# Down projection of the SwiGLU blocks: splits, sums and bank readings put in program order, readings moved directly behind their product

## The chip, the cores and the metric

The kernel runs on one core of one Trainium2 chip. The metric is device time in microseconds of that core, from launch to the last output; the time of a kernel is the median of its runs. The profile is one execution taken by the hardware profiler; its times count from the start of its span.

## The reference, cut to what matters

Two decoder layers, each a SwiGLU block, a mixer (attention and retention) and a second SwiGLU block, on 512 tokens of width 1024. The change lies in the SwiGLU block, which runs four times:

```python
D_MODEL = 1024; SEQ = 512; DEPTH = 2
D_FF = ((8 * D_MODEL // 3 + 127) // 128) * 128        # 2816

def swiglu_ffn(x, w_gu, w_down):
    a, u = jnp.split(x @ w_gu, 2, axis=-1)
    return (jax.nn.silu(a) * u) @ w_down

for l in range(DEPTH):
    x = layer_norm(ALPHA * x + 0.5 * swiglu_ffn(x, ffn1_w_gu[l], ffn1_w_down[l]), ln1_g[l], ln1_b[l])
    x = layer_norm(ALPHA * x + hybrid_mixer(x, w_in[l], w_out[l], ...), ln2_g[l], ln2_b[l])
    x = layer_norm(ALPHA * x + 0.5 * swiglu_ffn(x, ffn2_w_gu[l], ffn2_w_down[l]), ln3_g[l], ln3_b[l])
```

## The kernel before

**Three matmuls for one.** Every float32 operand is split into a high part (a copy to `float32r` on ScalarE, ACT) and a low part (operand minus high part, on VectorE, DVE); `split` issues the two. `mm3` then runs high x high, high x low and low x high on TensorE (PE). A split of 128x1024 is called a unit when it is of weights: tiles `uh` and `ul`. Units live in a pool of six (`UBUFS`).

**Where weights come from.** `Weights` holds the list of all units of the program. `get` hands the next one to PE; `done` gives a buffer back and calls `pump`, which emits loads (SP queue) and splits until six are held. So in the text of the program the split of unit i + 6 stands right behind the `done` of group i (numbered as below).

**The down projection.** Behind the gate and up projections a SwiGLU block multiplies its activations `hT` (22 blocks of 128 x 512 tokens) by the down weights, into eight PSUM banks. Blocks 0 to 15 go through a seven-product scheme (Strassen's), the others directly:

- The loop over `n` in `ffn` runs products n = 0 to 6 into the bank pairs left, low, high, low, right, low, low. Each has four groups `g`, each one unit and 12 matmuls of 128x512 (`seventh`). I number the groups i = 4n + g. Between n = 5 and n = 6 stands a direct `chunk` for block 16, whose last six matmuls add to the low banks; behind n = 6 chunk 17, then the tail (blocks 18 to 21, in tiles `hr`), whose first matmuls are followed by the layer norm.
- Weights of products: `down_items`. Products n = 1, 2, 3 and 6 use the same two tiles `R` (`R_311`, `R_312` in the first block): after the split of a group (`ul` on DVE has read it), POOL issues a DMA that adds the next block of weights onto the same half tile (L369), and the unit four places later (twelve from n = 3 to n = 6) is split from that sum; n = 4 and 5 do the same with two other tiles `R`. So unit i = 10 (`uh_341`, `ul_342`, n = 2, g = 2) needs the DMA that was issued behind unit i = 6 (`ul_332`).
- Activations of products: the generator `operands`. `operand` splits one 128x1024 piece into a quarter of `xh` and `xl`, which serves two groups. `fifth` (n = 2) first makes sums: s1 = a21 - a22, then a21 = a11 - a21 and a11 = s1 - a11 in place, and splits s1. `third` (n = 4) makes one sum. The list `ahead` keeps the operands three groups in front: the code that makes `fifth(0)`, used from i = 8, stands at i = 5; `fifth(1)`, used from i = 10, at i = 7; each behind the splits of unit i + 5 in the text (`ul_342` at i = 5, `ul_346` at i = 7).
- Readings: `into` adds a finished bank pair onto `Y` in SBUF (L726, two instructions). A bank may only be written again when it has been read.

**What sets the order.** Instructions go to each engine in an order that is fixed at build time; each engine then runs its own list from front to back. A scheduler may reorder what the program issued, except instructions for which `keep_in_program_order` was called. `self.pin` decides that in `split`; it is True at the start of the program and becomes False in the first SwiGLU block, at `fp == 0`. From there on only the POOL DMAs of L369 keep their place, and the scheduler places splits, sums and readings.

Of the kernel before, what the change touches and what calls it, by code (L numbers as in the profile page):

```python
# [7 lines left out]
F32 = mybir.dt.float32  # L8
F32R = mybir.dt.float32r
AF = mybir.ActivationFunctionType  # L10
ALU = mybir.AluOpType
# [18 lines left out]
GROUPS = 4  # L30
# [64 lines left out]
class Trunk:  # L95
# [57 lines left out]
    def units(self, pool=None, tag="u", bufs=None):  # L153
# [3 lines left out]
        lo = pool.tile([P, 1024], F32R, tag=tag + "l", name=self.nm("ul"), **kw)  # L157
        return hi, lo

    def split(self, hi, lo, src):  # L160
        a = self.nc.scalar.copy(hi, src)  # L161
        b = self.nc.vector.tensor_sub(lo, src, hi.bitcast(F32))  # L162
        if self.pin:
            self.tc.keep_in_program_order(a)
            self.tc.keep_in_program_order(b)

    def mm3(self, out, a, b, start, stop, **kw):
        (ah, al), (bh, bl) = a, b
# [313 lines left out]
    def ffn(self, g_, b, out=None):  # L482
        nc, tc, W = self.nc, self.tc, self.W
        with ExitStack() as ctx:
# [99 lines left out]
            for fp in range(NFP):  # L584
                if fp == 0:
# [4 lines left out]
                    more = []  # L590
# [46 lines left out]
            def part(m, i, j):  # L637

                f = (j * GROUPS + 2 * m) * 2
                return hT[:, f : f + 4, i * 256 : (i + 1) * 256]  # L640

            def operand(src):

                k = slots[0] = (slots[0] + 2) % KC
                f = src.shape[1]
                hh, hl = (v[:, k : k + 2, :].rearrange("p k t -> p (k t)").rearrange("p (f t) -> p f t", f=f)
                          for v in (self.xh, self.xl))
                self.split(hh, hl, src)
                h = f // 2
                return [(hh[:, q * h : q * h + h], hl[:, q * h : q * h + h]) for q in range(2)]  # L650

            s1 = pool.tile([P, 4, 256], F32, tag="tlh", name=self.nm("s1"), bufs=TAIL)

            def fifth(m):

                a11, a21, a22 = part(m, 0, 0), part(m, 1, 0), part(m, 1, 1)
                nc.vector.tensor_sub(s1, a21, a22)
                nc.vector.tensor_sub(a21, a11, a21)
                nc.vector.tensor_sub(a11, s1, a11)
                return operand(s1)  # L660

            def third(m):

                nc.vector.tensor_add(part(m, 0, 1), part(m, 0, 1), part(m, 0, 0))
                return operand(part(m, 0, 1))

            def operands():
                ms = range(GROUPS // 2)
                for m in ms[1:]:
                    yield from operand(part(m, 0, 1))  # L670
                for m in ms:
                    yield from operand(part(m, 0, 0))
                for m in ms:
                    yield from fifth(m)
                for m in ms:
                    yield from operand(part(m, 0, 0))
                for m in ms:
                    yield from third(m)
                for m in ms:
                    yield from operand(part(m, 1, 0))  # L680
                chunks = operand(hT[:, FIRST : FIRST + 2, :])
                yield chunks[0]
                for m in ms:
                    yield from operand(part(m, 1, 1))
                yield chunks[1]
                for f in range(NF - TAIL, NF, 2):
                    room = pool.tile([P, 2, 2, 512], F32R, tag="hr", name=self.nm("hr"), bufs=2)
                    self.split(room[:, 0], room[:, 1], hT[:, f : f + 2, :])
                    for q in range(2):
                        yield room[:, 0, q : q + 1], room[:, 1, q : q + 1]  # L690

            def seventh(banks, u, h, new):

                for i, b_ in enumerate(banks):
                    ts = slice(i * P, (i + 1) * P)
                    for f in range(2):
                        self.mm3(b_, (h[0][:, f, ts], h[1][:, f, ts]), (u[0][:, f, :], u[1][:, f, :]),
                                 new and f == 0, False, skip_group_check=True)
                self.step()

            def down(f, u, h, t, q):
# [2 lines left out]
                self.mm3(acc[t][q], (h[0][:, 0, ts], h[1][:, 0, ts]), (u[0][:, hs], u[1][:, hs]), False, f == NF - 1,  # L704
                         skip_group_check=True)

            split = operands()
            ahead = [(hv[0][:, g], hv[1][:, g]) for g in range(2)] + [next(split)]

            def chunk(f):  # L710
                u, h = W.get(), ahead.pop(0)
                ahead.append(next(split))
                for i, (t, q) in enumerate(((0, 0), (0, 1), (1, 0), (1, 1), (2, 1), (3, 1), (2, 0), (3, 0))):
                    down(f, u, h, t, q)
                    if i % 4 == 3:
                        self.step()
                W.done()
# [4 lines left out]
            def into(banks, t0, q, scale, sign=ALU.add):  # L722

                for i, b_ in enumerate(banks):
                    y = self.Y[:, t0 + i, q * 512 : (q + 1) * 512]
                    nc.vector.scalar_tensor_tensor(out=y, in0=y, scalar=scale, in1=b_, op0=ALU.mult, op1=sign)  # L726

            for n, (banks, new, more) in enumerate((
                    (left, True, None), (low, True, (0, 0, ALPHA)), (high, True, (0, 1, ALPHA)),
                    (low, False, (0, 1, 1.0, ALU.subtract)), (right, True, None),  # L730
                    (low, False, (2, 1, ALPHA, ALU.subtract)), (low, False, None))):
                if n == 6:
                    chunk(FIRST)
                for g in range(GROUPS):
                    u, h = W.get(), ahead.pop(0)
                    ahead.append(next(split))
                    seventh(banks, u, h, new and g == 0)
                    W.done(2 if n == 0 and g == 1 else 1)
                if more:
                    into(banks, *more)  # L740
            for f in range(FIRST + 1, NF - TAIL):
                if f == FIRST + 1:
                    gb = self.load_ln(self.spool, g_, b, "S", 2)
# [397 lines left out]
```

## Time and profile before

| what | value |
|---|---|
| median of 3 runs | 1791.03 us (1787.59 to 1792.43) |
| the profiled execution: its time / its span | 1792.29 us / 1790.4 us |
| busy in the span: DVE, ACT, POOL | 1386.6, 906.4, 162.7 us |
| granted TensorE clock, mean | 0.998 |
| first down projection (225 to 355 us): PE and DVE busy of 130 us | 127.99, 103.34 us |
| L726, reading of a bank | 32 times, 674 to 682 ns |
| L369, DMA issue on POOL | 64 times, 512 KB each |

How to read the rows below: in a timeline a row has start, duration (both us), engine, line, operation and tiles; the bracket at its end gives the idle time of the engine just before it and what was taken to end it. Buffer numbers are left out there, so `ul<-R,uh` is any weight unit split from a tile `R`. `PE ps L170` is the first matmul of `mm3`, L171 the second and L172 the third. In a list of waits: who waited for whom, us in total, times, longest us. The time from launch to span (1792.29 - 1790.4 = 1.9 us) is outside the rows.

### The profile page before, as it was taken

Reading aid. Unit: us, or ns where it says so; the run is one execution under the profiler, and the core shown is the slowest. Engines: PE = TensorE matmul, PEld = TensorE weight load, DVE = VectorE, ACT = ScalarE, POOL = GpSimd, SP = SyncE. Lnnn points to the kernel's source line nnn. Section 1 sums busy time; section 2 is a strip of 40 time slices with the busy share of each in tenths; the row PEclk is TensorE's granted clock in tenths of the full one; section 3 lists DMA queues with packets and bytes.
Section 4 is the critical chain, followed back from the end, with each engine's and each line's share of the span. In section 5 each row is a group of like instructions: output and inputs, shape, how many; then the busy total and the mean of one; then the engine's idle time right before and its main releaser. Section 6 shows DMA issues by size and latency. Waiting matters only on the chain.

```text
span 1790.4 us, 29087 instructions
## 1 busy us (share of the span) xinstructions
PE 1767.3 (99%) x11978; PEld 1611.0 (90%) x11978; DVE 1386.6 (77%) x1926; ACT 906.4 (51%) x1423; POOL 162.7 (9%) x136
## 2 busy tenths in 40 slices
PE   9999999999999999999999999999999999999998
PEld 9999987887789999998799999889877899999876
DVE  7888888656767888879688887877667687888884
ACT  5455555278722455556235555553785234555550
POOL 0000031111111000012000000301011100000211
PEclk9999999999999999999999999999999999999999
DMA  6234397223222232389313324961323122244961
GB/s 188 95 102 135 120 228 172 88 83 90 52 95 71 86 127 95 95 241 181 118 58 98 106 95 165 224 175 42 99 79 94 48 95 95 95 129 131 217 136 48
DMA packets 158326, 210.07 MB, mean 117 GB/s; under 512 B 4848, under 2 KB 116208, under 8 KB 158192
## 3 DMA queue, kind: packets, MB, share of 16 engines
q1 hardware_dynamic: 140784, 174.64, 30.3%
q0 software_dynamic: 17408, 33.56, 10.5%
q8 instruction: 94, 1.54, 0.4%
q14 instruction: 40, 0.33, 0.1%
HBM read 206.09 MB, written 2.10 MB: 116 GB/s over the span
## 4 chain that ended last, share of the span: by engine, by line
PE 73%; DVE 10%; issue 7%; DMA 4%; ACT 4%; POOL 1%; SPq 0%; POOLq 0%; DVEq 0%; ACTq 0%
PE ps L170 23%; PE ps L171 23%; PE ps L172 23%; DVE ul L162 4%; DMA R<-in_ffn_w_down_dram 2%; DVE xl L162 2%; ACT uh L161 1%; PE ps L435 1%; DMA raw<-in_ffn_w_down_dram 1%; ACT sw L910 1%; DMA raw<-in_ffn_w_gu_dram 1%; ACT b L952 1%; ACT b L946 1%; DVE Y L726 1%; POOL R L369 0%
## 5 line engine op out<-in xcount | busy, mean ns | idle before, releaser
L170 PE MATMUL ps<-xh,uh 128*128 128x256 f32 (+1 forms) x1616 | 482.1, 298 | 0.0
L172 PE MATMUL ps<-xh,ul 128*128 128x256 f32 (+1 forms) x1616 | 479.1, 297 | 0.9 <-DVE ul L162 0.9
L171 PE MATMUL ps<-xl,uh 128*128 128x256 f32 (+1 forms) x1616 | 478.7, 296 | 0.2 <-DVE xl L162 0.2
L161 ACT CAST uh<-raw 128x1024 fp32r<-128x1024 f32 (+1 forms) x285 | 249.2, 894 | 247.9 <-PE ps L171 136.8
L162 DVE TENSOR_TENSOR ul<-raw,uh 128x1024 fp32r<-128x1024 f32 (+1 forms) x285 | 287.6, 1024 | 87.8 <-ACT uh L161 87.5
L170 PE MATMUL ps<-Th,uh 128*128 128x256 f32 x1152 | 319.1, 277 | 0.0
L171 PE MATMUL ps<-Tl,uh 128*128 128x256 f32 x1152 | 318.7, 277 | 0.0
L172 PE MATMUL ps<-Th,ul 128*128 128x256 f32 x1152 | 318.3, 276 | 0.0
L170 PEld LDWEIGHTS ps<-xh,uh 128*128 128x128 f32 x1616 | 307.9, 191 | 10.5 <-issue 1.6
L172 PEld LDWEIGHTS ps<-xh,ul 128*128 128x128 f32 x1616 | 307.8, 191 | 9.8 <-DVE ul L162 1.3
L171 PEld LDWEIGHTS ps<-xl,uh 128*128 128x128 f32 x1616 | 308.0, 191 | 8.4 <-DVE xl L162 0.8
L170 PE MATMUL ps<-uh,xh 128*128 128x512 f32 x672 | 265.1, 394 | 8.2 <-DVE Y L726 8.2
L171 PE MATMUL ps<-ul,xh 128*128 128x512 f32 x672 | 262.2, 390 | 0.0
L172 PE MATMUL ps<-uh,xl 128*128 128x512 f32 x672 | 261.9, 390 | 0.0
L161 ACT CAST uh<-S 128x1024 fp32r<-128x1024 f32 x144 | 151.2, 1050 | 149.0 <-PE ps L171 145.1
L162 DVE TENSOR_TENSOR ul<-S,uh 128x1024 fp32r<-128x1024 f32 x144 | 175.9, 1221 | 60.1 <-ACT uh L161 59.5
L171 PEld LDWEIGHTS ps<-Tl,uh 128*128 128x128 f32 x1152 | 216.7, 188 | 0.0
L170 PEld LDWEIGHTS ps<-Th,uh 128*128 128x128 f32 x1152 | 216.7, 188 | 0.0
L172 PEld LDWEIGHTS ps<-Th,ul 128*128 128x128 f32 x1152 | 216.3, 188 | 0.0
L369 POOL DMA_DIRECT2D R<-in_ffn_w_down_dram x64 | 77.7, 1216 | 994.7 <-DVE ul L162 959.0
L170 PEld LDWEIGHTS ps<-uh,xh 128*128 128x128 f32 x672 | 126.5, 188 | 38.2 <-DVE Y L726 9.9
L172 PEld LDWEIGHTS ps<-uh,xl 128*128 128x128 f32 x672 | 126.4, 188 | 26.6
(143 smaller groups left out, 2391.5 us busy)
## 6 DMA issues: line engine op xcount, KB each, us to landing
raw<-in_ffn_w_gu_dram SPq DMA_DIRECT2D x86, 1024.0 KB, 5.4
R<-in_ffn_w_down_dram POOLq DMA_DIRECT2D x64, 512.0 KB, 7.4
raw<-in_ffn_w_down_dram SPq DMA_DIRECT2D x20, 1024.0 KB, 5.1
raw<-in_w_in_dram SPq DMA_DIRECT2D x18, 1024.0 KB, 5.2
R<-in_ffn_w_down_dram SPq DMA_DIRECT2D x16, 1024.0 KB, 6.4
raw<-in_w_in_dram SPq DMA_DIRECT2D x8, 512.0 KB, 4.6
raw<-in_w_out_dram SPq DMA_DIRECT2D x8, 512.0 KB, 6.2
raw<-in_w_out_dram SPq DMA_DIRECT2D x4, 1024.0 KB, 4.9
```

Source lines behind the costliest of these rows:

```text
L161: a = self.nc.scalar.copy(hi, src)
L162: b = self.nc.vector.tensor_sub(lo, src, hi.bitcast(F32))
L170: mm(out, ah, bh, start=start, stop=False, **kw)
L171: mm(out, ah, bl, start=False, stop=False, **kw)
L172: mm(out, al, bh, start=False, stop=stop, **kw)
L369: self.nc.gpsimd.dma_start(src, rows(i, j, g * 256, 256), accum_op=ALU.add))
L435: nc.tensor.transpose(b[:, c * P : (c + 1) * P], src[:, c * P : (c + 1) * P], self.ident)
L726: nc.vector.scalar_tensor_tensor(out=y, in0=y, scalar=scale, in1=b_, op0=ALU.mult, op1=sign)
L910: nc.scalar.copy(sw[q * 32 : q * 32 + 32, :n], src[o * 32 : o * 32 + 32, :n])
L946: nc.scalar.activation(s[kv][:, cc, :nk], s[kv][:, cc, :nk], AF.Exp, bias=m[:, cc : cc + 1], scale=SCALE, accum_out=den[:, cc : cc + 1])
L952: nc.scalar.activation(s[kv][:, cc, :nk], s[kv][:, cc, :nk], AF.Copy, scale=den[:, cc : cc + 1])
```

## The change

`pin` is set to True ahead of the loop over `n` and back to False behind it, so that within the seven products every split, every sum of activations and every reading keeps the program's place. `fifth`, `third` and `into` call `keep` for this. And `into` moves from behind the last group's `W.done` to before it, that is ahead of the split that this `done` emits.

```diff
+    def keep(self, ins):
+        if self.pin:
+            self.tc.keep_in_program_order(ins)
+
     def split(self, hi, lo, src):
-        a = self.nc.scalar.copy(hi, src)
-        b = self.nc.vector.tensor_sub(lo, src, hi.bitcast(F32))
-        if self.pin:
-            self.tc.keep_in_program_order(a)
-            self.tc.keep_in_program_order(b)
+        self.keep(self.nc.scalar.copy(hi, src))
+        self.keep(self.nc.vector.tensor_sub(lo, src, hi.bitcast(F32)))
...
             def fifth(m):
...
-                nc.vector.tensor_sub(s1, a21, a22)
-                nc.vector.tensor_sub(a21, a11, a21)
-                nc.vector.tensor_sub(a11, s1, a11)
+                for out, p_, q_ in ((s1, a21, a22), (a21, a11, a21), (a11, s1, a11)):
+                    self.keep(nc.vector.tensor_sub(out, p_, q_))
                 return operand(s1)
...
-                nc.vector.tensor_add(part(m, 0, 1), part(m, 0, 1), part(m, 0, 0))
+                self.keep(nc.vector.tensor_add(part(m, 0, 1), part(m, 0, 1), part(m, 0, 0)))
...
+            self.pin = True
             split = operands()
...
-                    nc.vector.scalar_tensor_tensor(out=y, in0=y, scalar=scale, in1=b_, op0=ALU.mult, op1=sign)
+                    self.keep(nc.vector.scalar_tensor_tensor(out=y, in0=y, scalar=scale, in1=b_, op0=ALU.mult,
+                                                             op1=sign))
...
                     seventh(banks, u, h, new and g == 0)
+                    if more and g == GROUPS - 1:
+                        into(banks, *more)
                     W.done(2 if n == 0 and g == 1 else 1)
-                if more:
-                    into(banks, *more)
+            self.pin = False
             for f in range(FIRST + 1, NF - TAIL):
```

No instruction is added or removed; orders change on DVE, ACT and SP, and by one matmul per SwiGLU block on PE. POOL's order stays. The three places below are in the first SwiGLU block; the other three have the same rows with other buffer numbers.

**DVE around the first sum of `fifth`.** `ul_318` to `ul_344` are units i = 4 to 11, L657 to L659 the sums, `xl_78<-s1` the low part of the first operand of n = 2. Before:

```order
L162 TENSOR_TENSOR xl_78<-hT_14_145,xh_77 128x1024
L162 TENSOR_TENSOR ul_318_2767<-R_311_2700,uh_317_2766 128x1024
L657 TENSOR_TENSOR s1_328_2786<-hT_14_145 128x1024
L162 TENSOR_TENSOR ul_330_2802<-R_311_2700,uh_329_2801 128x1024
L658 TENSOR_TENSOR hT_14_145<-hT_14_145 128x4x256
L162 TENSOR_TENSOR ul_332_2821<-R_312_2702,uh_331_2820 128x1024
L162 TENSOR_TENSOR ul_334_2826<-R_312_2702,uh_333_2825 128x1024
L659 TENSOR_TENSOR hT_14_145<-s1_328_2786,hT_14_145 128x4x256
L162 TENSOR_TENSOR xl_78<-s1_328_2786,xh_77 128x1024
L162 TENSOR_TENSOR ul_336_2843<-R_311_2700,uh_335_2842 128x1024
L162 TENSOR_TENSOR ul_340_2866<-R_311_2700,uh_339_2865 128x1024
```

Of the change, from `ul_334` on (the sums are all on L659 there):

```order
L166 TENSOR_TENSOR ul_334_2826<-R_312_2702,uh_333_2825 128x1024
L166 TENSOR_TENSOR ul_336_2843<-R_311_2700,uh_335_2842 128x1024
L166 TENSOR_TENSOR xl_78<-hT_14_145,xh_77 128x1024
L166 TENSOR_TENSOR ul_340_2866<-R_311_2700,uh_339_2865 128x1024
L166 TENSOR_TENSOR ul_342_2883<-R_312_2702,uh_341_2882 128x1024
L659 TENSOR_TENSOR s1_328_2786<-hT_14_145 128x1024
L659 TENSOR_TENSOR hT_14_145<-hT_14_145 128x4x256
L659 TENSOR_TENSOR hT_14_145<-s1_328_2786,hT_14_145 128x4x256
L166 TENSOR_TENSOR xl_78<-s1_328_2786,xh_77 128x1024
L166 TENSOR_TENSOR ul_344_2905<-R_312_2702,uh_343_2904 128x1024
L166 TENSOR_TENSOR ul_346_2922<-R_311_2700,uh_345_2921 128x1024
```

Before, the first sums and `xl_78<-s1` stand between the units i = 4 to 7 and ahead of `ul_336`; in the change they stand behind `ul_342`, and the second set of sums and its `xl_78<-s1` directly behind `ul_346`. The `xl_78<-hT` that stood directly ahead of `ul_318` stands behind it in the change.

**DVE around the reading of product n = 5.** `ul_372` to `ul_378` are the units of n = 6, `ul_380` chunk 17, `ul_383` to `ul_391` and `hr` the tail. Before:

```order
L162 TENSOR_TENSOR hr_389_3302<-hT_14_145,hr_389_3302 128x1024
L162 TENSOR_TENSOR ul_370_3145<-raw_308_2671,uh_369_3144 128x1024
L162 TENSOR_TENSOR hr_396_3343<-hT_14_145,hr_396_3343 128x1024
L162 TENSOR_TENSOR xl_78<-hT_14_145,xh_77 128x1024
L162 TENSOR_TENSOR ul_372_3163<-R_311_2700,uh_371_3162 128x1024
L162 TENSOR_TENSOR ul_374_3179<-R_311_2700,uh_373_3178 128x1024
L162 TENSOR_TENSOR xl_78<-hT_14_145,xh_77 128x1024
L162 TENSOR_TENSOR ul_376_3197<-R_312_2702,uh_375_3196 128x1024
L162 TENSOR_TENSOR ul_378_3215<-R_312_2702,uh_377_3214 128x1024
L726 SCALAR_TENSOR_TENSOR Y_79<-Y_79,ps_324_2782 128x512
L726 SCALAR_TENSOR_TENSOR Y_79<-Y_79,ps_326_2784 128x512
L162 TENSOR_TENSOR ul_380_3231<-raw_308_2671,uh_379_3230 128x1024
```

Of the change:

```order
L166 TENSOR_TENSOR ul_378_3215<-R_312_2702,uh_377_3214 128x1024
L727 SCALAR_TENSOR_TENSOR Y_79<-Y_79,ps_324_2782 128x512
L727 SCALAR_TENSOR_TENSOR Y_79<-Y_79,ps_326_2784 128x512
L166 TENSOR_TENSOR ul_380_3233<-raw_308_2671,uh_379_3232 128x1024
L166 TENSOR_TENSOR xl_78<-hT_14_145,xh_77 128x1024
L166 TENSOR_TENSOR ul_383_3265<-raw_315_2737,uh_382_3264 128x1024
L166 TENSOR_TENSOR ul_385_3281<-raw_315_2737,uh_384_3280 128x1024
L166 TENSOR_TENSOR ul_388_3299<-raw_381_3236,uh_387_3298 128x1024
L166 TENSOR_TENSOR hr_389_3302<-hT_14_145,hr_389_3302 128x1024
L166 TENSOR_TENSOR ul_391_3318<-raw_381_3236,uh_390_3317 128x1024
L166 TENSOR_TENSOR hr_396_3343<-hT_14_145,hr_396_3343 128x1024
```

The reading stands behind `ul_378` in both. But the six splits of the tail (`ul_383`, `ul_385`, `ul_388`, `ul_391`, two `hr`), which before stood ahead of the reading, among the units of n = 4 and n = 5, now stand behind it.

**SP's loads around the tail.** `raw_381` holds the down weights of the last two tail units, `raw_386` and `raw_392` the first weights of the next stage, `ln` the norm's constants. Before:

```order
L358 DMA R_338_2846<-in_ffn1_w_down_dram 128x4x512
L267 DMA raw_381_3234<-in_ffn1_w_down_dram 128x2x1024
L191 DMA raw_386_3284<-in_w_in_dram 128x8x256
L448 DMA ln_395_3340<-in_ln1_g_dram 128x1024
L449 DMA ln_395_3340<-in_ln1_b_dram 128x1024
L229 DMA raw_392_3321<-in_w_in_dram 128x8x128 x2
```

Of the change:

```order
L359 DMA R_338_2846<-in_ffn1_w_down_dram 128x4x512
L449 DMA ln_395_3340<-in_ln1_g_dram 128x1024
L450 DMA ln_395_3340<-in_ln1_b_dram 128x1024
L268 DMA raw_381_3236<-in_ffn1_w_down_dram 128x2x1024
L192 DMA raw_386_3284<-in_w_in_dram 128x8x256
L230 DMA raw_392_3321<-in_w_in_dram 128x8x128 x2
```

The loads of `raw_381` and `raw_386` moved behind those of `ln`; `raw_381` now takes the buffer that `ul_380` leaves, where before it took the one that `ul_385` left.

## The prediction

> **What bounds the kernel now.** I read the page's busy times first, then the list of waits for PE, then the timeline at each of them.
>
> ```profile
> span 1790.4 us, 29087 instructions
> PE 1767.3 (99%) x11978; PEld 1611.0 (90%) x11978; DVE 1386.6 (77%) x1926; ACT 906.4 (51%) x1423; POOL 162.7 (9%) x136
> PE ps L170 <- DVE Y L726: 8.2, 4, 3.5
> ```
>
> PE is busy for 1767.3 of 1790.4 us, so a change of order can win little and lose more: work in front of PE counts only where PE stands still. Half of what PE waits for is one line: four times, once per SwiGLU block, a bank had not been read by L726 when PE came back to it. On PE, first block, then the others:
>
> ```profile
> 302.62 0.39 PE L172 MATMUL ps<-uh,xl 128*128 128x512 f32 x1
> 305.02 0.50 PE L170 MATMUL ps<-uh,xh 128*128 128x512 f32 x1 [2.01 <-DVE Y L726]
> 305.36 0.39 PE L171 MATMUL ps<-ul,xh 128*128 128x512 f32 x1
> 855.11 0.50 PE L170 MATMUL ps<-uh,xh 128*128 128x512 f32 x1 [2.04 <-DVE Y L726]
> 1189.63 0.50 PE L170 MATMUL ps<-uh,xh 128*128 128x512 f32 x1 [0.69 <-DVE Y L726]
> 1737.32 0.39 PE L172 MATMUL ps<-uh,xl 128*128 128x512 f32 x1
> 1741.21 0.80 PE L170 MATMUL ps<-uh,xh 128*128 128x512 f32 x1 [3.50 <-DVE Y L726]
> 1741.80 0.63 PE L171 MATMUL ps<-ul,xh 128*128 128x512 f32 x1
> ...
> 1744.59 0.40 PE L172 MATMUL ps<-uh,xl 128*128 128x512 f32 x1
> ```
>
> The reader is to see the starts. With the start of the stage at 233.47 (quoted below), the 306th matmul starts at 302.62: a step of 69.15 / 305 = 0.2267 us. In the first block the step of the wait is 2.40, and the next 0.34, together 2.28 too long, 0.27 more than the idle time in the bracket. Added to the brackets of the second and third block that makes 2.31 and 0.96. In the fourth, nine steps take 7.27 instead of 2.04: 5.23 lost, of which 3.5 is the wait; the rest is the clock:
>
> ```profile
> 853.00:855.00 2.00, 0.07 (x1) 0.00 (x0) 2.00 (x4) 0.00 (x0) 0.00 (x0) 1.00 0.98 309
> 1742.00:1744.00 2.00, 2.00 (x7) 1.52 (x6) 0.89 (x1) 0.00 (x0) 0.00 (x0) 0.50 0.00 0
> ```
>
> In these windows (length, then busy PE, PEld, DVE, ACT, POOL, then the granted clock) the clock stays 1.00 in a wait of 2 us and falls to 0.50 behind the one of 3.5. The late readings cost 2.28 + 2.31 + 0.96 + 5.23 = **10.8 us**: the most that the change can win.
>
> **First term, the reading.** Before, the reading of n = 5 is late because DVE is behind with its list:
>
> ```profile
> 304.29 1.27 DVE L726 SCALAR_TENSOR_TENSOR Y<-Y,ps 128x512 f32<-128x512 f32 x2
> ```
>
> Product n = 5 ended at 233.47 + 288 x 0.2267 = 298.8, PE comes back to its banks 18 matmuls (4.1 us) later, and the readings start only at 304.29. Six splits that stood ahead move behind, at 1.135 us a step (rows below) 6.8 us, more than the reading is late. Nothing else ahead of it in the new list is late, and once the product ends the two readings need some 1.3 of the 4.1 us. So the four waits go: -10.8.
>
> **Second term, what the program's order holds up.** The sums of `fifth` and `xl<-s1` stood early in DVE's list; now they stand behind `ul_342`, whose high part waits for a DMA. The start of the stage on PE in the four blocks, and the start of this high part (`uh_341` and its likes) on ACT:
>
> ```profile
> 233.47 0.39 PE L170 MATMUL ps<-uh,uh 128*128 128x512 f32 x1
> 783.53 0.39 PE L170 MATMUL ps<-uh,uh 128*128 128x512 f32 x1
> 1119.40 0.39 PE L170 MATMUL ps<-uh,uh 128*128 128x512 f32 x1
> 1668.17 0.39 PE L170 MATMUL ps<-uh,uh 128*128 128x512 f32 x1
> ```
>
> ```profile
> 247.32 1.05 ACT L161 CAST uh<-R 128x1024 fp32r<-128x1024 f32 x1 [4.26 <-PE ps L172]
> 249.87 1.05 ACT L161 CAST uh<-R 128x1024 fp32r<-128x1024 f32 x1 [1.50 <-DMA R<-in_ffn_w_down_dram]
> 252.49 1.05 ACT L161 CAST uh<-R 128x1024 fp32r<-128x1024 f32 x1 [1.57 <-DMA R<-in_ffn_w_down_dram]
> 803.32 1.05 ACT L161 CAST uh<-R 128x1024 fp32r<-128x1024 f32 x1 [1.49 <-DMA R<-in_ffn_w_down_dram]
> 1138.17 1.05 ACT L161 CAST uh<-R 128x1024 fp32r<-128x1024 f32 x1 [1.57 <-DMA R<-in_ffn_w_down_dram]
> 1688.22 1.05 ACT L161 CAST uh<-R 128x1024 fp32r<-128x1024 f32 x1 [2.66 <-DMA R<-in_ffn_w_down_dram]
> ```
>
> I call this start U, counted from the stage's: 19.02, 19.79, 18.77 and 20.05 us. (At 247.32 the page names PE, but unit i = 8 needs PE only up to group 2, done at 241.6; so there too it was the DMA.) DVE's durations and steps:
>
> ```profile
> 248.41 1.23 DVE L162 TENSOR_TENSOR ul<-R,uh 128x1024 fp32r<-128x1024 f32 x1 [3.47 <-ACT uh L161]
> 252.09 1.22 DVE L657 TENSOR_TENSOR s<-hT 128x1024 f32<-128x1024 f32 x1
> 253.23 1.22 DVE L664 TENSOR_TENSOR hT<-hT 128x1024 f32<-128x1024 f32 x1
> 254.36 1.22 DVE L162 TENSOR_TENSOR ul<-R,uh 128x1024 fp32r<-128x1024 f32 x1
> ```
>
> A low part starts 1.09 behind its high part (247.32 to 248.41); neighbours on DVE start 1.135 apart; each lasts 1.22. So in the change `ul_342` starts at U + 1.09, three sums and `xl<-s1` follow, and that ends at U + 1.09 + 4 x 1.135 + 1.22 = U + 6.85. PE wants it for the third matmul of i = 8, at 98 x 0.2267 = 22.2. It waits U - 15.4: 3.7 us in the first block. Behind it stand `ul_344`, `ul_346`, the second three sums and the second `xl<-s1`, six steps or 6.8 us, so this one ends at U + 13.66; PE wants it for the fourth matmul of i = 10 (the scheduler put one other ahead of it there), at 123 x 0.2267 = 27.9. The second wait thus adds 1.1, and the whole delay is **D = U - 14.2**: 4.8, 5.6, 4.55 and 5.85, sum 20.8 us, with the landing of before.
>
> Can the landing come earlier? The DMAs behind units i = 4, 6 and 7 are issued on POOL at:
>
> ```profile
> 237.33 1.35 POOL L369 DMA_DIRECT2D R<-in_ffn_w_down_dram  x1 [236.02 <-DVE ul L162]
> 241.83 1.20 POOL L369 DMA_DIRECT2D R<-in_ffn_w_down_dram  x1 [1.05 <-DVE ul L162]
> 247.50 1.23 POOL L369 DMA_DIRECT2D R<-in_ffn_w_down_dram  x1 [4.47 <-DMA R<-in_ffn_w_down_dram]
> ```
>
> And of these issues in the first block (shortest, middle, longest):
>
> ```profile
> DMA to landing us min/median/max: 5.7/7.4/10.6
> ```
>
> They land 2.6 us apart (247.32, 249.87, 252.49), whatever the gaps of issue, and the fourth waits until the first has landed: a saturated queue. The first issue moves up by one step at most, 1.1 us (one split less ahead of `ul_318`); the third hardly, since `uh_331` waits for PE. So U falls by 0 to 1.1; I take 0.4, nearer to the third's own, and the sum becomes 20.8 - 1.6 = **+19.2**. The far bound is a landing 5.7 behind the issue, U = 241.83 + 5.7 - 233.47 = 14.1: no wait at all.
>
> Smaller effects: the operand of i = 6 now stands behind `ul_336` and ends at 247.32 + 1.09 + 1.135 + 1.22 = 250.8 or up to 1.1 earlier, wanted at 250.2; a wait there only takes from the one behind it, which the DMA sets. Behind the second wait DVE needs two readings (some 0.6 each), two units and a split, 4.6 us, and PE 5.2 until it wants that split: 0.6 to spare, nothing lost. From n = 4 on the margins grow to over 1 us, as PE has become later.
>
> **Third term, the tail.** Six splits and the loads of `raw_381` and `raw_386` come later on ACT, DVE and SP.
>
> ```profile
> 322.82 0.39 PE L170 MATMUL ps<-uh,hr 128*128 128x512 f32 x1
> 324.10 1.23 DVE L162 TENSOR_TENSOR ul<-raw,uh 128x1024 fp32r<-128x1024 f32 x1 [4.18 <-ACT uh L161]
> raw<-in_ffn_w_down_dram SPq DMA_DIRECT2D x20, 1024.0 KB, 5.1
> ```
>
> With PE later by D - 2.3 = 2.1, the tail starts at 324.9. `ul_380` can run when group 23 is done, 298.8 + 4.4, and with `uh_379` and the queue ends near 306; the load of `raw_381` then lands at 311.5, and its two splits and the two `hr` end near 317. That is 7.6 us early. The mixer's six units follow it; DVE has idle time there (4.18 us ahead of 324.10 alone), and the norm behind waits for PE. I set nothing; should the load land over 7 us late, that falls on PE. POOL's own list keeps its order.
>
> **The sum**: -10.8 + 19.2 = +8.4 us on the profiled execution's 1792.29 (span 1790.4 and 1.9 around it): 1800.7. The median of the runs, 1791.03, lies 1.3 lower, so 1799.5.
>
> **Rivals.** (1) The landing is early and the change wins. Place: the DMA behind `ul_332`. It decides at D = 2.7 per block, U = 16.9, 1.9 below the earliest U of before; with U under 15.4 no first wait is left and the time is 1780 to 1785. For it: the 5.7 of the fastest landing. Against it: four blocks, all at 18.8 to 20.05. (2) A wash, U near 16.9, by loads that spread otherwise: 1786 to 1796. (3) The clock falls at the new wait. In the first block PE stands 1.4 us for `xh<-s1` (ready 4.6 behind U), does two matmuls, then stands 1.8 for `xl`. In the rows 2.0 left the clock at 1.00 and 3.5 halved it, at a price of 5.23 - 3.5 - 0.2 = 1.5. Halved, PE loses 1.5 ahead of i = 10 in place of the 1.1 of the second wait: 0.4 a block, 1.7 in all, 1801.2; where a second drop follows it is up to 1806. The Trainium skill, "TensorE: Matmul & The Clock Gate", "What's actually happening", has the clock halve after an idle window of about 3.4 us that runs freely, and come back after as long a busy one; the trace agrees (1.00 behind 2.0 us idle, 0.50 behind 3.5). By it neither piece alone halves the clock, and the sum stays as it is. (4) The reading stays late, as its neighbour ahead is `ul_378` in both lists: then nothing is won, 1810. Against it: 6.8 us of work have left the list ahead.
>
> **How the numbers follow.** The forecast has 0.58, (3) 0.13, (1) 0.11, (2) 0.14, (4) 0.04. No change of under 0.3%, 5.4 us, can be told from none. Forecast, (3) and (4) are slower by more, 0.75; (2) is the same, 0.14; (1) faster, 0.11. The range takes the forecast with D between U unchanged and 1.1 earlier (1796.6 to 1801.1), the clock up to 1806, and of (2) most: 1789 to 1806. It leaves out (1) and (4).
>
> **What would show it.** In the profile of the change: no wait of PE for L726's line; four pairs of new waits of PE for DVE `xl`, about 3 us at the first groups of n = 2 and about 1 two groups on, with `xl<-s1` ending some 6.9 us behind the `uh` that waited for its DMA; the tail without a wait. I am wrong if that `uh` starts less than 17 us behind the stage's first matmul, if the sums run ahead of it after all, or if PE waits for the tail's splits or the norm.

## The result, and the profile after

The change is slower: 1810.51 us, the median of 6 runs (1809.06 to 1815.21), beside 1791.73 of before (6 runs, 1787.59 to 1797.67); ratio 1.0108, 95% interval 1.0087 to 1.013. The prediction had 1799.5, range 1789 to 1806: the direction was right, the size was not.

The profiled execution of the change took 1809.06 us. Span and busy times from its page, then the first rows of the waits for PE:

```profile
span 1807.3 us, 29071 instructions
PE 1776.1 (98%) x11978; PEld 1614.2 (89%) x11978; DVE 1391.2 (77%) x1926; ACT 908.8 (50%) x1423; POOL 162.8 (9%) x136
```

```profile
PE ps L173 <- DVE xl L166: 8.6, 7, 1.8
PE ps L171 <- ACT xh L165: 6.7, 6, 2.1
```

The wait for the reading, 8.2 us before, is gone from the list. In its place PE waits for the two parts of activation operands. PE is also busy 8.8 us longer (1776.1 against 1767.3) with the same matmuls, so some of them ran slower.

To see where the time lies I measure the **stage**: from the first matmul of the seven products (`ps<-uh,uh`) to the first one of the tail (`ps<-uh,hr`), 384 matmuls, at 0.2267 us each 87.05 us. The prediction quotes the four starts of before and its first tail; its other three tails, from the timeline of PE:

```profile
872.93 0.39 PE L170 MATMUL ps<-uh,hr 128*128 128x512 f32 x1
1207.48 0.39 PE L170 MATMUL ps<-uh,hr 128*128 128x512 f32 x1
1760.46 0.39 PE L170 MATMUL ps<-uh,hr 128*128 128x512 f32 x1
```

The same of the change, starts and tails:

```profile
233.63 0.39 PE L171 MATMUL ps<-uh,uh 128*128 128x512 f32 x1
327.03 0.39 PE L171 MATMUL ps<-uh,hr 128*128 128x512 f32 x1
787.92 0.39 PE L171 MATMUL ps<-uh,uh 128*128 128x512 f32 x1
882.94 0.39 PE L171 MATMUL ps<-uh,hr 128*128 128x512 f32 x1
1130.02 0.39 PE L171 MATMUL ps<-uh,uh 128*128 128x512 f32 x1
1222.92 0.39 PE L171 MATMUL ps<-uh,hr 128*128 128x512 f32 x1
1683.97 0.39 PE L171 MATMUL ps<-uh,uh 128*128 128x512 f32 x1
1777.34 0.39 PE L171 MATMUL ps<-uh,hr 128*128 128x512 f32 x1
```

Lengths before: 89.35, 89.40, 88.08, 92.29, together 359.1. After: 93.40, 95.02, 92.90, 93.37, together 374.7. So 15.6 of the 16.9 us between the two spans lie inside the stages, and 1.3 outside. Above the floor (4 x 87.05 = 348.2) the stages lost 10.9 before and 26.5 now.

Where inside: the first block on PE, from the timeline (idle time just before, and its releaser, in brackets), with the two waits of block 2 at unit i = 18 as the last rows:

```profile
256.74 0.50 PE L171 MATMUL ps<-uh,xh 128*128 128x512 f32 x1 [1.17 <-ACT xh L165]
257.08 0.40 PE L172 MATMUL ps<-ul,xh 128*128 128x512 f32 x1
259.32 0.79 PE L173 MATMUL ps<-uh,xl 128*128 128x512 f32 x1 [1.84 <-DVE xl L166]
259.91 0.63 PE L171 MATMUL ps<-uh,xh 128*128 128x512 f32 x1
...
843.91 0.50 PE L171 MATMUL ps<-uh,xh 128*128 128x512 f32 x1 [0.71 <-ACT xh L165]
845.17 0.50 PE L173 MATMUL ps<-uh,xl 128*128 128x512 f32 x1 [0.53 <-DVE xl L166]
```

The first two waits are those at i = 8 that the prediction named, in all four blocks (idle 1.17, 2.13, 1.27 and 0.94 for `xh`, 1.84 each time for `xl`; with PE's restart, the 0.1 to 0.3 us by which the steps at and behind a wait exceed its idle time, 14.6 us in all). Behind them matmuls start 0.43 apart in place of 0.2267 (a matmul lasts 0.63 there, not 0.39). Granted clock in the same stretch, cut where it changes (length, busy time of PE, PEld, DVE, ACT, POOL, then the clock):

```profile
254.93:258.35 3.42, 1.37 (x5) 0.48 (x3) 3.35 (x4) 2.71 (x3) 1.12 (x1) 1.00 1.14 208
258.35:261.76 3.41, 2.44 (x6) 1.96 (x7) 3.41 (x4) 0.23 (x1) 0.94 (x1) 0.50 1.07 196
265.17:268.59 3.42, 3.42 (x17) 2.79 (x16) 3.42 (x6) 2.48 (x3) 0.00 (x0) 1.00 1.09 193
```

It fell at 258.35, while PE stood in the second wait, and was back at 265.17. The clock halved in all four blocks, which cost 7.65 us of slow steps; the second wait, forecast at i = 10, does not appear. At i = 18 PE waits again, 3.74 us in all: 0, 1.78, 0.46 and 1.50 by block, counted with PE's restart and the steps between the two waits. That place was not in the sum. In all: 14.6 + 7.65 + 3.74 = 26.0 of the 26.5; the rest is the restart behind the second wait, 0.11 a block.

The cause of the waits at i = 8, on ACT and then on DVE, first block:

```profile
252.17 1.05 ACT L165 CAST uh<-R 128x1024 fp32r<-128x1024 f32 x1 [1.55 <-DMA R<-in_ffn_w_down_dram]
255.64 1.04 ACT L165 CAST xh<-s 128x1024 fp32r<-128x1024 f32 x1 [2.43 <-DVE s L659]
```

```profile
253.25 1.23 DVE L166 TENSOR_TENSOR ul<-R,uh 128x1024 fp32r<-128x1024 f32 x1 [1.37 <-ACT uh L165]
254.39 1.22 DVE L659 TENSOR_TENSOR s<-hT 128x1024 f32<-128x1024 f32 x1
255.64 1.23 DVE L659 TENSOR_TENSOR hT<-hT 128x1024 f32<-128x1024 f32 x1
256.90 1.22 DVE L659 TENSOR_TENSOR hT<-s,hT 128x1024 f32<-128x1024 f32 x1
258.05 1.22 DVE L166 TENSOR_TENSOR xl<-s,xh 128x1024 fp32r<-128x1024 f32 x1
```

This is the chain as predicted: `uh` waits for its DMA, `ul` follows 1.08 later, then three sums and `xl<-s`, which ends at 259.27; PE's third matmul starts at 259.32.

### The profile page after: what moved, and what is told of

It is laid out like the page before. It is cut to its first block, busy times and chain, and to the rows that moved or that the text cites. A ratio compares the mean times of both kernels' runs of the same rounds, so it can differ in the third digit from the quotient of the medians.

```text
span 1807.3 us, 29071 instructions
## 1 busy us (share of the span) xinstructions
PE 1776.1 (98%) x11978; PEld 1614.2 (89%) x11978; DVE 1391.2 (77%) x1926; ACT 908.8 (50%) x1423; POOL 162.8 (9%) x136
## 4 chain that ended last, share of the span: by engine, by line
PE 36%; DVE 6%; issue 4%; DMA 2%; ACT 2%; POOL 1%; POOLq 0%; DVEq 0%; SPq 0%; ACTq 0%
PE ps L173 12%; PE ps L171 12%; PE ps L172 12%; DMA R<-in_ffn_w_down_dram 2%; DVE ul L166 1%; DVE xl L166 1%; DVE Y L472 1%; DVE st L462 1%; DVE Y L469 1%; ACT sw L913 1%; DVE Y L460 0%; POOL sw L915 0%; ACT uh L165 0%; PE ps L436 0%; DVE hT L659 0%
```

## The experiments

The runs were made in three series, each beside runs of the kernel before on the same chip: its medians there are 1794.15 (19 runs), 1793.11 (13) and 1792.86 (13). The ratios of e1 to e9 are to those.

| run | time, us | ratio (95%) | four stages | rest of span |
|---|---|---|---|---|
| before | 1791.73 | 1 | 359.1 | 1431.3 |
| the change | 1810.51 | 1.0108 (1.0087 to 1.013) | 374.7 | 1432.6 |
| e1_filler | 1810.59 | 1.009 (1.0074 to 1.0105) | 376.7 | 1432.3 |
| e2_operands_free | 1783.75 | 0.9945 (0.993 to 0.9959) | 348.2 | 1435.8 |
| e3_ahead_4 | 1794.3 | 1.0005 (0.9995 to 1.0014) | 359.6 | 1431.9 |
| e4_ahead_5 | 1789.56 | 0.9976 (0.9966 to 0.9986) | 348.2 | 1437.5 |
| e5_readings_alone | 1792.63 | 0.9998 (0.9982 to 1.0013) | 355.7 | 1430.8 |
| e6_no_move | 1806.14 | 1.0077 (1.0048 to 1.0105) | 372.6 | 1432.0 |
| e7_tail_free | 1818.86 | 1.0155 (1.0126 to 1.0184) | 386.1 | 1431.7 |
| e8_fifth_free | 1793.55 | 0.9996 (0.9983 to 1.001) | 359.9 | 1432.8 |
| e9_third_ahead | 1804.91 | 1.0066 (1.0042 to 1.0091) | 369.8 | 1431.9 |

The last two columns are of the profiled execution; the rest is its span less its stages.

**e1_filler: is the halved clock what is lost?** Twelve more matmuls just ahead of i = 8 fill PE's idle time; they go into a bank that the fifth product starts anew, so their values are never used.

```diff
                     ahead.append(next(split))
                     seventh(banks, u, h, new and g == 0)
+                    if n == 2 and g == 0:
+                        for _ in range(12):
+                            nc.tensor.matmul(right[0], last[0][:, 0, :P], u[0][:, 0, :], start=True, stop=True)
+                    last = h
```

> The change, with 12 matmuls of 128x512 (2.7 us) put in front of the first group of n = 2, on data that is there, into a bank that product n = 4 overwrites; they leave the output as it is. If the idle time of PE at n = 2 halves the clock, and the halved clock costs more than the second wait that it hides: clock 1.00 in the four stages, the slow matmuls behind the wait gone (7.6 us in all), a second wait of about 1.1 us per block two groups on in their place, time 3 us below the change (1810.5 -> 1807.5). If the slow matmuls have another cause: they stay, and the 12 matmuls either hide in the wait (1810) or add up to 10.9 us (1821).

The slow steps are gone (clock 0.999), and the 3 us that were expected are not won: the four stages are 93.62, 94.86, 92.90 and 95.33 long, together 376.7 against 374.7, and by the ratios, 1.009 and 1.0108, the two kernels can't be told apart. What came in place of the slow steps, on PE in the first block (at i = 10; the other three have 1.32, 1.33 and 1.28):

```profile
266.01 0.50 PE L173 MATMUL ps<-uh,xl 128*128 128x512 f32 x1 [1.32 <-DVE xl L166]
```

The second wait, 1.59 a block with its restart and 6.3 in all, is back where the slow steps took 7.65, and i = 18 rises from 3.74 to 5.7, which takes the difference back. A halved clock ahead of a wait costs only what it takes beyond that wait.

**e2_operands_free: only the activations' sums and splits are not kept.**

```diff
-            split = operands()
+            def free(gen):
+                while True:
+                    was, self.pin = self.pin, False
+                    x = next(gen, None)
+                    self.pin = was
+                    if x is None:
+                        return
+                    yield x
+
+            split = free(operands())
```

> The change, but the operands of the products (the sums of activations and their splits) are left to the scheduler; units and readings keep the program's order. If the loss comes from the operand of n = 2 standing behind a unit that waits for its DMA: no wait of PE at n = 2 and none two products later, clock 1.00, and of the readings' four waits only the last block's in part (four of the six tail splits stand ahead of the reading again, 2.3 us less work than before): 1781 to 1784, 8 to 11 us below before. If the loss comes from the pinned units or readings, or from the later loads of the tail: near the change, 1805 to 1812.

As expected. No stage is over 87.08 us long: no wait for an operand, none for a reading (a part of the last block's was expected to stay). It is faster than both kernels. On DVE, first block, around the first `xl<-s`:

```profile
248.62 1.22 DVE L166 TENSOR_TENSOR xl<-s,xh 128x1024 fp32r<-128x1024 f32 x1
250.02 1.23 DVE L166 TENSOR_TENSOR ul<-R,uh 128x1024 fp32r<-128x1024 f32 x1 [0.17 <-ACT uh L165]
```

This stage starts at 232.49, so `xl<-s` starts 16.1 us into it, in the change 258.05 - 233.63 = 24.4. It stands two units ahead of `ul_342` (the row at 250.02 is `ul_340`). The whole loss in the stages thus comes from holding the operands' work in the program's place. Four of the tail's six splits also moved ahead of the reading of n = 5 here, yet PE didn't wait for it. Some of the gain is given back outside the stages (1435.8 against 1431.3): from the tails to the next stages 5.5 us are lost, 5.1 of them behind the second. There the norm starts 8.8 us behind the tail's first matmul, as two splits of the next stage's weights stand ahead of it, and PE later stands 3.05 us for an operand's low part, and the clock halves.

**e3_ahead_4 and e4_ahead_5: the order is kept, but operands are made one or two groups earlier.** The first list holds two or three calls in place of one; in e4 the generator may run out (`next(split, None)`).

```diff
-            ahead = [(hv[0][:, g], hv[1][:, g]) for g in range(2)] + [next(split)]
+            ahead = [(hv[0][:, g], hv[1][:, g]) for g in range(2)] + [next(split) for _ in range(2)]
```

> The change, with operands made four groups ahead of their use, not three, so that fifth(0) stands behind unit i = 9. By my formula its low part ends 6.85 us behind that unit's start (16.4, 17.2, 16.2 and 16.3 us from the stage's first matmul): 23 to 24 us, wanted at 22.2; a first wait of 0.8 to 1.9 us and a second of about 1.1 two groups on, no halved clock since neither reaches 2 us: 2 to 3 us per block, 9 in all, against 10.8 won at the readings: 1789 to 1792. If the place of the operands is not the cause: 1808 to 1812.

> The change, with operands made five groups ahead, so that fifth(0) stands behind unit i = 8 and fifth(1) behind i = 10. Low parts then end at 13.9 + 6.85 = 20.7 us (wanted at 22.2) and 18.8 to 20.1 + 6.85 = 25.7 to 26.9 us (wanted at 27.9): no wait at n = 2, none at n = 4, no wait for readings, clock 1.00: 1780 to 1783, faster than both kernels. If the place of the operands is not the cause: 1808 to 1812.

In e3 both waits at n = 2 remain, at `xl` alone; on PE, first block:

```profile
255.24 0.50 PE L173 MATMUL ps<-uh,xl 128*128 128x512 f32 x1 [0.66 <-DVE xl L166]
262.30 0.50 PE L173 MATMUL ps<-uh,xl 128*128 128x512 f32 x1 [1.30 <-DVE xl L166]
```

They are 0.93 and 1.58 with restarts (1.99 and 1.59 in the second block), the clock stays up, and i = 18 is free of waits. In e4 all stages are at 87.05 or 87.06, as expected. Both missed in time: e3 is as fast as before and not a little faster, and e4's 1789.56 is well above the 1780 to 1783 that its stages alone would give. The rest of its span grew by 6.2 us over before, 5.6 of it between a tail's first matmul and the next stage (462.25, 248.57 and 462.67, where before has 460.71, 246.47 and 460.69). PE's waits in the stages behind, from its list, are for low parts of activations:

```profile
PE ps L172 <- DVE xl L166: 3.7, 5, 1.5
```

The norm on DVE in its first block:

```profile
324.72 2.36 DVE L166 TENSOR_TENSOR ul<-raw,uh 128x1024 fp32r<-128x1024 f32 x2 [1.18 <-ACT uh L165]
327.00 0.68 DVE L460 SCALAR_TENSOR_TENSOR Y<-Y,ps 128x512 f32<-128x512 f32 x1
```

The tail's first matmul is at 321.10 there. The norm's first instruction follows two splits of the next stage's weights without idle time, 5.9 us behind the tail's start. Before it came 2.9 behind (322.82 to 325.75) and waited for PE:

```profile
325.75 0.69 DVE L459 SCALAR_TENSOR_TENSOR Y<-Y,ps 128x512 f32<-128x512 f32 x1 [0.42 <-PE ps L172]
```

**e5_readings_alone and e6_no_move: does the reading's own place matter?** e5 is the kernel before with only the readings moved and kept. e6 is the change with the move undone:

```diff
-                    if more and g == GROUPS - 1:
-                        into(banks, *more)
                     W.done(2 if n == 0 and g == 1 else 1)
+                if more:
+                    into(banks, *more)
```

> The kernel before, with nothing changed but the readings: into stands ahead of the last group's done and its two instructions keep the program's place. Splits and sums are placed by the scheduler as before, so the six splits of the tail stay ahead of the reading of n = 5. Theory (the 10.8 us of late readings are due to those six splits, and the move of the reading by itself does nothing, its neighbour being ul_378 either way): PE still waits four times for the reading, about 8 us in all, no wait behind fifth appears, and the time is that of before within 4 us: 1790 to 1798 beside a kernel before at 1794. Rival (the reading's own place or its keep is what takes the wait away): no wait of PE for the reading, stages of 87 us, about 1783.

> The change without the move: splits, sums and readings keep the program's order, but into stands behind the last group's done, so each reading comes one split (1.1 us) later on DVE. Theory (the reading has some 2 us of slack once the tail's splits are gone, and the loss is that of fifth behind its DMA): no wait of PE for the readings, the same two waits at n = 2 and those at i = 18, 1808 to 1813. Rival (the move is part of the gain, the splits alone would not free the bank in time): four waits of PE for the reading of about 1 us, 1812 to 1816.

Of e5, from the list of waits:

```profile
PE ps L170 <- DVE Y L727: 6.2, 4, 1.8
```

The four waits stay in e5 (6.2 us in this execution, 8.2 in that of before), and the time is that of before. e6 has no wait for a reading, and is no slower than the change; its 1806.14 is 1.9 below the range that was expected, and its stages are 2.1 shorter than the change's. So neither the move nor the readings' own `keep` takes the wait away.

**e7_tail_free: e4 with the tail's splits not kept.** The first piece is in the split of the tail's weight units, the second in that of its activations.

```diff
+                was, self.pin = self.pin, self.pin and pools[c] is None
                 self.split(hi, lo, v[:, c, :])
+                self.pin = was
...
+                    was, self.pin = self.pin, False
                     self.split(room[:, 0], room[:, 1], hT[:, f : f + 2, :])
+                    self.pin = was
```

> The version with operands made five groups ahead (1789.6 us), in which the four tail units and the two hr splits are not kept, so that they and the loads behind them stand as early as before. One low part of the tail then stands among the second sums of fifth and waits for a load: up to 2 us at i = 10 in each block is possible. Theory (the 5.6 us that this version lost outside the products come from the tail's splits and loads being late, so that the next stage's splits stand ahead of the norm on DVE): from the tail's first matmul to the next stage 460.7, 246.5 and 460.7 us again in place of 462.25, 248.57 and 462.67, and 1784 to 1786 where no wait appears at i = 10, up to 1791 where it does. Rival (the loss outside lies elsewhere, in the start of the program or the mixer): those three times stay at 462 and 248.5, 1789 or more.

Far slower than expected: the place at i = 10 was named in the expectation, at far too low a price, and the waits for the reading were not in it. DVE in the first block, and then PE, with the reading's wait of the second block as the last row:

```profile
262.08 1.23 DVE L166 TENSOR_TENSOR ul<-raw,uh 128x1024 fp32r<-128x1024 f32 x1 [2.20 <-ACT uh L165]
...
264.36 1.22 DVE L166 TENSOR_TENSOR xl<-s,xh 128x1024 fp32r<-128x1024 f32 x1
...
310.35 1.22 DVE L166 TENSOR_TENSOR hr<-hT,hr 128x1024 fp32r<-128x1024 f32 x1
311.48 1.22 DVE L166 TENSOR_TENSOR ul<-R,uh 128x1024 fp32r<-128x1024 f32 x1
312.62 1.27 DVE L731 SCALAR_TENSOR_TENSOR Y<-Y,ps 128x512 f32<-128x512 f32 x2
```

```profile
263.05 0.50 PE L171 MATMUL ps<-uh,xh 128*128 128x512 f32 x1 [2.19 <-ACT xh L165]
265.63 0.79 PE L173 MATMUL ps<-uh,xl 128*128 128x512 f32 x1 [1.85 <-DVE xl L166]
313.35 0.79 PE L171 MATMUL ps<-uh,xh 128*128 128x512 f32 x1 [2.92 <-DVE Y L731]
...
873.92 0.50 PE L171 MATMUL ps<-uh,xh 128*128 128x512 f32 x1 [3.26 <-DVE Y L731]
```

A split of the tail that waits for its load stands among the second sums; with the slow matmuls behind the waits it costs 7.4 us at i = 10 in this block (24.0 over the four; up to 2 a block was expected). And with tail splits on DVE ahead of the reading of n = 5, PE waits for that reading again in every block: 2.92, 3.26, 2.64 and 1.03 us of idle time, where e4 had none. On the question it was made for it decides little. The times from tail to next stage are 460.78, 246.47 and 460.97, within 0.3 of their old values as its theory had it, but PE came to the tail 6.8 to 13.5 us later into the stage than in e4, so the norm had slack either way.

**e8_fifth_free and e9_third_ahead: the waits at n = 2 and at i = 18 apart.** e8 is the change with only `fifth` not kept; e9 is the change with operands one group earlier from i = 12 on.

```diff
                 for m in ms:
-                    yield from fifth(m)
+                    self.pin = False
+                    made = fifth(m)
+                    self.pin = True
+                    yield from made
```

```diff
-                    ahead.append(next(split))
+                    ahead += [next(split) for _ in range(2 if (n, g) == (3, 0) else 1)]
```

> The change, but the sums and splits of fifth alone (n = 2) are not kept; those of third (n = 4), all units and all readings keep the program's order. On DVE the first xl<-s1 moves from behind ul_342 to ahead of it, the sums spread among the units before; the list around n = 4 is unchanged. Theory (third(1) behind ul_362 and its DMA is a second case of the same mechanism, with a price of its own): no wait of PE at n = 2, but waits at i = 18 of 0.5 to 2.5 us in each block, stages of 87.5 to 89.5 us, 1786 to 1792. Rival (the waits at i = 18 are only what the delay of n = 2 leaves behind): none at i = 18, stages of 87.1 us, 1782 to 1785.

> The change, with operands made one group earlier from i = 12 on (n = 3), and as before up to there. So third(1) stands behind unit 19 in place of unit 20, and fifth stays behind its DMA. Theory (second term and i = 18 are two prices): waits at n = 2 and the slow matmuls as in the change, none at i = 18, stages shorter by 0, 1.8, 0.5 and 1.5, 1805 to 1808. Rival (the wait at i = 18 only takes up what would be waited for later anyway, at n = 5 or the tail): the stage's lengths stay at 93 to 95 and the time at 1809 to 1812.

e8, the only waits of PE inside its first stage (which starts at 234.15):

```profile
284.61 0.50 PE L171 MATMUL ps<-uh,xh 128*128 128x512 f32 x1 [1.28 <-ACT xh L165]
285.87 0.50 PE L173 MATMUL ps<-uh,xl 128*128 128x512 f32 x1 [0.53 <-DVE xl L166]
```

and on ACT, with the unit i = 20 that waits for its DMA, ahead of the operand:

```profile
280.04 1.05 ACT L165 CAST uh<-R 128x1024 fp32r<-128x1024 f32 x1 [2.72 <-DMA R<-in_ffn_w_down_dram]
283.51 1.04 ACT L165 CAST xh<-hT 128x1024 fp32r<-128x1024 f32 x1 [2.43 <-DVE hT L664]
```

No wait at n = 2 is left, but i = 18 now costs 2.36 in the first two blocks, 2.13 and 2.50 in the others (counted as for the change), and 1.6 more in the third, where the clock halves: it is a price of its own, and larger when PE comes in time. The stages are 14.8 us shorter than the change's; 1793.55 is 1.6 above the expected range. e9 has no wait at i = 18 and keeps those at n = 2: its stages are 4.9 shorter than the change's, at 1804.91, 0.1 below the expected range. Of that, 3.6 are in the three blocks that had waited at i = 18; 1.3 are in the first, where the clock stayed up. So that wait did not merely take up a later one.

## Why the prediction missed, step by step

Two steps of it failed: the margins from n = 4 on, where it set nothing and PE waits 3.74 us at i = 18, and the second wait at i = 10, 4.8 us in the sum, where the clock fell and slow steps took 7.65; with the clock up (e1) that wait takes 6.3. The rest of the span adds 1.3.

**First term, the reading: right.** No wait for it is left. Its reason (six splits of the tail ahead of the reading) has two runs behind it: with the readings moved and kept alone (e5) the waits stay, and with tail splits brought back ahead (e7) the waits come back, though DVE is late there for the load too. e2 adds a limit: four of the six ahead did no harm there.

**Second term at i = 8: right, in place, chain and size.** 14.6 us measured, the restart behind the second wait left out; U - 15.4 a block, with the landing 0.4 earlier, gives 14.4. Two errors cancel in it. The landing moved up by more than I took: this `uh` starts 18.54 behind the stage's start in the first block and (ACT's timeline: 807.42, 1148.65, 1702.27) 19.50, 18.63 and 18.30 in the others, 74.97 together against 77.63 before, 0.67 a block. And a sum that overwrites what the one ahead of it reads steps 1.25 (254.39 to 255.64), not 1.135.

**Second term at i = 10: mis-sized, and overlaid by rival (3).** I had 1.2 a block (D less the first wait). e1, where the clock stays up, shows 1.59: the two sums that step 1.25 add 0.23, and PE's restarts about 0.2. In the change itself the clock fell in all four blocks, to which I gave 0.13, and the slow steps took 7.65 where the second wait had 4.8 in the sum: 2.85 too little. The prediction read "neither piece alone halves the clock" from a page of the Trainium skill ("TensorE: Matmul & The Clock Gate", "What's actually happening"), which has the clock halve after an idle window of about 3.4 us that runs freely. The traces agree that the window runs freely: within each trace, the changes of the granted clock lie whole multiples of 3.413 us apart (in the change it falls at 258.35, 814.72, 1156.05 and 1709.01), and each low stretch inside the stages lasts 3.41 or 6.83. They differ on how idle such a window must be, and there the traces decide. Cut along these marks, the windows at whose end the clock fell in the change held 2.04, 2.53, 2.43 and 2.37 us of idle time, not 3.4 (first block: 3.42 less PE's 1.37 in the row at 254.93). In e9's first block nearly the same two waits as in the change's, 1.19 and 1.85 us, are cut by a mark into 1.47 and 1.57, and the clock stayed up:

```profile
254.31:257.72 3.41, 1.94 (x8) 0.96 (x6) 3.34 (x4) 2.11 (x3) 1.20 (x1) 1.00 1.12 205
257.72:261.14 3.42, 1.85 (x8) 1.54 (x9) 3.42 (x4) 0.83 (x1) 0.35 (x1) 1.00 1.14 208
```

So what counts is the idle time inside one window, not the length of a piece; my error was to judge the pieces one by one. The price of 1.5 for a halved stretch was that of one window; the first block had two (258.35 to 265.17). But e1 shows that this is not where the 8 us went: with the clock up, the waits at i = 10 and 18 sum to 6.3 + 5.7 = 12.0, against 7.65 + 3.74 = 11.4 in the change.

**The smaller effects: this step failed.** "From n = 4 on the margins grow to over 1 us, as PE has become later." The same mechanism as at n = 2 stands there a second time: `third(1)`, used from i = 18, behind unit i = 20 (`ul_362`), whose high part waits for its DMA. It costs 3.74 us in the change, and 9.4 in e8 (11.0 with slow steps), where nothing else delays PE. The margin doesn't grow with PE's lateness since the DMA comes later too. This `uh` starts 280.04 - 234.15 = 45.9 into the first stage in e8 and 46.1 into the second, and in the change, from ACT's timeline, blocks 1 and 2:

```profile
282.95 1.05 ACT L165 CAST uh<-R 128x1024 fp32r<-128x1024 f32 x1 [1.88 <-DMA R<-in_ffn_w_down_dram]
839.34 1.05 ACT L165 CAST uh<-R 128x1024 fp32r<-128x1024 f32 x1 [3.12 <-DMA R<-in_ffn_w_down_dram]
```

That is 49.3 and 51.4. By the steps ahead of i = 18, PE was late by 6.3 and 6.2 us there, and the DMA by 3.4 and 5.3. I take it that PE's lateness comes back through the units' buffers, DVE's splits and the issues behind them; that path I have argued, not tried apart. Only what is left of the lateness, 2.9 and 0.9 us, helps PE, and in e8, without any, PE is short by 2.4: that leaves no wait in block 1 and some 1.5 in block 2, where 1.78 was measured.

**Third term, the tail: nearly right, for a wrong reason.** PE doesn't wait for the tail's own splits. But outside the stages 1.3 us were lost (1432.6 against 1431.3). In the change too the norm stands behind next-stage splits:

```profile
328.65 2.36 DVE L166 TENSOR_TENSOR ul<-raw,uh 128x1024 fp32r<-128x1024 f32 x2 [0.83 <-ACT uh L165]
330.93 0.68 DVE L460 SCALAR_TENSOR_TENSOR Y<-Y,ps 128x512 f32<-128x512 f32 x1
```

That is 3.9 behind the tail's start in place of 2.9. "The norm behind waits for PE" held before and no longer holds; that this makes the 1.3 is not shown. Where PE comes early, this order costs more: 5.6 in e4 and 5.5 in e2, both with waits of PE for the next stage's operands. Whether the splits' place or the later loads on SP bring it about was not separated: e7, made for that, hid it.

**The sum.** Of the 8.4 us between 1800.7 and the profiled 1809.06: slow steps in place of the second wait 2.85, i = 18 3.74, the rest of the span 1.3, the first wait and the restarts behind the second piece 0.6; together 8.5. The other 2.7 us of the miss are runs: I took the median 1.3 below the profiled execution, and it lies 1.45 above.

**The rivals.** (1), (2) and (4) did not occur. (3) did, but its "1801.2" assumed one slow stretch a block of 1.5, where 1.9 were measured, and no wait at i = 18.

## What to carry to other kernels

Keeping the program's order on an engine that runs its list from front to back puts every instruction behind the slowest wait ahead of it: list each kept instruction that waits for a DMA, and every operand behind it, not only the first such place. Keep what needs the order (here the units: with the readings alone kept, in e5, PE still waits, and with the units kept too, in e2, it does not) and leave free, or issue earlier, what feeds PE: e2 does the first and beats both kernels by 0.55% and 1.5%, and e4 does the second. A margin against a DMA whose issue depends on the late engine must not be counted as growing with the lateness.

## What the runs showed of the hardware

TensorE's clock is granted by windows of 3.413 us that run on whatever PE does. Over the eleven traces, counting windows in which the clock was up and PE's idle time by the profile's (modelled) ends of matmuls: all 26 windows with 1.97 us of idle time or more were followed by a halved clock, none with 1.57 or less, and of those between, 3 were and 8 were not. It came back behind windows with at most 0.41 us of idle time and stayed low behind those with 0.73 or more. So the place of a wait in the windows decides too, not its length alone: in e7 one wait of 3.26 us (at 873.92) left the clock at 1.00, as a mark cut it and the two windows had 1.75 and 1.51 of idle time, while one of 2.92 (at 313.35) halved it, with 2.19 in one window.

In e1, with the idle time filled, the clock stayed at 0.999 in the mean and the stages were no shorter: slow matmuls whose successor has to wait for an operand are nearly free.

A sum on DVE that overwrites what the sum directly ahead of it reads starts 1.25 us behind it (254.39 to 255.64, 255.64 to 256.90), where other neighbours start 1.135 apart. It was seen in the sums of `fifth` alone; what in them costs the 0.12 was not tried.
